# Stores of a decayed cumulative matmul: two queues for four lumps near the end, and half-size stores for the last chunk's lower lump

## The chip, the cores and the metric

The kernel runs on one core of a Trainium2 chip. The time is the device time of one execution in microseconds (us). Five engines work side by side, each in the order of its own instructions: TensorE (PE, with its weight loads as PEld), VectorE (DVE), ScalarE (ACT), GpSimd (POOL) and SyncE (SP). SP here only issues stores. DMAs issued by SP go through one queue (q1 in the profile), those issued by GpSimd through another (q0). SP's issues are not counted as busy time of an engine; GpSimd's are.

## What is computed

```
xw = x @ w                       # x: 16 x 2048 x 1024, w: 1024 x 1024, float32
out[:, 0, :] = xw[:, 0, :]
for t in range(1, S):            # S = 2048
    out[:, t, :] = decay * out[:, t - 1, :] + xw[:, t, :]
```

So each row of x is multiplied by w, and along the 2048 steps of a sequence each of the 1024 columns keeps a running sum that decays by its own factor.

## The kernel before

The 16 sequences are cut into 64 chunks of 512 steps. Two chunks make a group, except that the last two chunks (62 and 63) stand alone. For each group the 1024 output columns are cut into 8 tiles of 128, so there are 31 x 8 slots of 1024 steps and then 2 x 8 of 512 steps: 264 slots in all. The text counts the last ones from the end: slots -24 to -17 are the last group of two chunks, -16 to -9 are chunk 62, and -8 to -1 are chunk 63.

What one slot does, with the letters of the written order:

- TensorE computes the tile's matmuls into PSUM (`ps` or `spare`, L131), columns on the partitions and steps along the row. Eight matmuls of 512 steps take 1.73 us.
- A **paired** tile is scanned at half length. ScalarE copies PSUM to `xs` (p, L183) and scales its even steps (g, L169). GpSimd adds these to the odd steps: the **join** (j, L196). VectorE scans the odd steps with the squared decay (S, L201) into `so`. ScalarE scales the result (h, L169), and GpSimd adds it to the even steps: the **fill** (c, L246). A small write sets the element ahead of the first step, the **zero** (z): a memset on GpSimd at a sequence's start (L190), a copy on ScalarE otherwise (L192).
- A tile that isn't paired is scanned by VectorE straight from PSUM (S, L221). A list `flips` says for which slots the usual choice is turned round; of the last eight, -8, -6, -3, -2 and -1 aren't paired.
- The last column of `so` is kept for the next chunk (k, L250).
- VectorE transposes the tile into the output buffer `ot` in blocks of 32 x 32 (B for back, L258).

Four tiles share one `ot` buffer, and there are four such buffers in a ring. A buffer with its four tiles is a **lump** here: half of the columns, for one group or chunk. When the last of the four transposes has been put in the program, `Outlet.store` issues the lump's stores (L279), one for each quadrant of 32 partitions, in the order 0, 2, 1, 3. A store of a two-chunk lump is 512 KB, one of a single chunk 256 KB. Each moves pieces of 512 bytes, 1024 or 512 of them.

The last four tiles (-4 to -1) have no such buffer. Their end is the deed `V`: TensorE transposes them in blocks of 128 steps (L383), ScalarE and VectorE copy two blocks each out of PSUM (L387), and SP stores each block, 128 rows of 2 KB (L389).

The order of the instructions is the order in which the program is written; `pin` keeps it. For the first 34 slots and the last 20 it is written out by hand in `agenda`, one string of deeds for a slot, where `S-13` is the scan of slot -13; the slots between follow a rule (`usual`, `rest`). A deed that touches several engines puts one instruction in each one's order. A `B` that completes a lump also puts the lump's stores there, and each waits for the lump's last transpose on VectorE.

Loads of x are issued by GpSimd (L105), 256 KB each and 128 KB for the first two chunks, and are cast to bf16 on the way. The last one is issued at 824.5 us.

Of the kernel before, what the change touches and what calls it, by code (L numbers as in the profile page):

```python
# [14 lines left out]
def _ap(ap_obj: bass.AP, new_ap, extra_offset=0):  # L15
    return dataclasses.replace(
        ap_obj,
        ap=[list(p) for p in new_ap],
        offset=ap_obj.offset + extra_offset,
    )  # L20
# [5 lines left out]
def kernel(  # L26
# [26 lines left out]
    nc = tc.nc  # L53
    pin = tc.keep_in_program_order
    B, S, D = x.shape
# [3 lines left out]
    P = 32  # L59
# [6 lines left out]
    R = K // 2  # L66
    CH = D // 2
    CR = CH // NQ
# [7 lines left out]
    def ring(pool, name, count, shape, dtype=FP32):  # L76
        i = turns[name] = turns.get(name, -1) + 1
        return pool.tile(shape, dtype, name=f"{name}{i % count}")

    def quad(q):  # L80
        return slice(q * P, (q + 1) * P)
# [12 lines left out]
    def ot_tile(nj):  # L94
        return ring(sb, "ot", 4, [128, nj, CR])
# [29 lines left out]
    def matmul(ps, n, k, xt, t0=0, t1=TL, start=0, pairs=None):  # L125
        if pairs is None:
            rhs = xt[:, k // 2, k % 2, t0:t1]
        else:
            rhs = pairs[:, k // 2, t0 // P:t1 // P, :, k % 2].rearrange("p j i -> p (j i)")
        lhs = wsb[:, k, n].rearrange("p q i -> p (q i)")  # L130
        pin(nc.tensor.matmul(  # L131
            out=ps[:, t0:t1] if ps.shape[1] >= t1 else ps,
            lhsT=lhs,
            rhs=rhs,
            start=(k == 0 and t0 == start),
            stop=(k == K - 1),
        ))
# [3 lines left out]
    class Tile:  # L141
# [3 lines left out]
        def __init__(self, g, n, ps, outlets):  # L145
            self.b, self.t0 = chunks[g[0]]
            self.T = TL * len(g)
            self.n, self.ps, self.outlets = n, ps, outlets
            self.paired = n % R != R - 1
            if len(tiles) in flips or len(tiles) - len(slots) in flips:  # L150
                self.paired = not self.paired
            self.turn = len(tiles)
            self.lot = sum(t.paired for t in tiles)
            self.prev = None if self.t0 == 0 else last[n]
            if self.t0 + self.T < S:
                last[n] = const.tile([128, 1], FP32, name=f"keep{n}", bufs=2)
                self.keep = last[n]
            else:
                self.keep = None
# [106 lines left out]
    class Outlet:  # L266


        def __init__(self, ns, nj, half=0, queues=(nc.sync,)):
            self.ns, self.missing, self.half = ns, set(ns), half  # L270
            self.nj, self.t0, self.queues = nj, half * nj * P, queues
            self.ot = ot_tile(nj)

        def store(self, b, t0):
            n0 = self.ns[0]
            c0 = n0 % R * P
            size = len(self.ns) * P
            for i, q in enumerate((0, 2, 1, 3)):
                pin(self.queues[i % len(self.queues)].dma_start(  # L279
                    out=_ap(out, [[D, P], [P * D, self.nj], [1, size]],  # L280
                            (b * S + t0 + self.t0) * D + n0 // R * CH + q * CR + c0),
                    in_=self.ot[quad(q), :, c0:c0 + size]))

# [1 line left out]
    size = M * CH  # L287
# [37 lines left out]
    for q in range(NQ):  # L325
        pin(nc.sync.dma_start(
            out=rows[q * P:q * P + R],
            in_=_ap(decay, [[P, R], [CH, 2], [1, P]], q * CR)))
# [75 lines left out]
    def turn_and_load(c):  # L404
# [77 lines left out]
        -17: "h-20 k-20 c-20 S-18 k-18",  # L482
        -16: "I S-17 B-20 p-16 g-16 j-16",
        -15: "z-15 k-17 B-18 z-16",
        -14: "p-15 g-15 B-17 z-14 j-15",
        -13: "p-14 S-16 g-14 j-14 S-15 h-16 k-16 c-16",
        -12: "S-13 h-15 k-15 c-15 S-14 k-13",
        -11: "p-12 B-13 h-14 B-15 g-12 c-14 k-14 B-16",
# [1 line left out]
        -9: "p-10 k-12 g-10 h-12 B-11 j-10 k-11",  # L490
        -8: "S-9 c-12 S-10 k-9",
        -7: "z-7 B-12 h-10 k-10 B-9 c-10 S-8",
        -6: "p-7 g-7 B-10 j-7 B-8",
        -5: "S-7 S-6 h-7 c-7",
        -4: "z-4 S-5 B-7",
        -3: "p-4 B-6 g-4 B-5 j-4",
# [13 lines left out]
    def usual(s):  # L510
        paired = [t.paired for t in tiles]
        do = [f"P{s}"] if paired[s] else []
        if paired[s - 1]:
            do.append(f"S{s - 1}")
        if not paired[s]:
            do.append(f"S{s}")
        do.append(f"C{s - 1}")
        if paired[s - 2]:
            do.append(f"B{s - 2}")
        if not paired[s - 1]:  # L520
            do.append(f"B{s - 1}")
        return do + later.get(s, []) + ["L"] * (2 if len(loads) > NQ else 1)

    def rest(s):
        do = [f"S{s - 1}"] if tiles[s - 1].paired else []
        do.append(f"C{s - 1}")
        if tiles[s - 2].paired:
            do.append(f"B{s - 2}")
        return do + [f"B{s - 1}"] + later.get(s, []) + ["L"] * len(loads)

    def perform(do):
        for deed in do:
            deeds[deed[0]](int(deed[1:] or 0))
# [3 lines left out]
    for step, (g, n) in enumerate(slots):  # L537
        T = TL * len(g)
        left = step - len(slots)
        if n % R == 0:  # L540
            ns, nj = range(n, n + R), T // P
            outlets = [Outlet(ns, nj)]
        if left == -R:
            outlets = []
        if step == 0:
            heads = [ring(psp, "ps", 3, [128, T]) for _ in range(3)]
            firsts = [ps[:, 0:TL] for ps in heads] + [spares[0]]
            seconds = [ps[:, TL:T] for ps in heads] + [spares[1]]
            for j0, j1 in halves:
                for k in range(0, K, 2):  # L550
                    for i in range(R):
                        matmul(firsts[i], i, k, xt_of[0], j0 * P, j1 * P, pairs=xw_of[0])
            for k in range(1, K, 2):
                for i in range(R):
                    matmul(firsts[i], i, k, xt_of[0])
            for k0 in range(0, K, 2):
                for i in range(R):
                    for k in (k0, k0 + 1):
                        matmul(seconds[i], i, k, xt_of[1], 0, H * P,
                               pairs=xw_of[1] if k0 < 4 else None)  # L560
            for i in range(R):
                for k in range(K):
                    matmul(seconds[i], i, k, xt_of[1], H * P, TL, H * P,
                           pairs=xw_of[1] if i < 2 else None)
        if step < R:
            ps = heads[n] if n < 3 else tuple(spares)
        else:
            if step == K + 1:
                ps = nexts
            elif len(g) == 2 or n % R < 3:  # L570
                ps = ring(psp, "ps", 3, [128, T])
            else:
                ps = ring(psp, "spare", 1, [128, TL])
            todo = [(k, l) for k in range(K) for l in range(len(g))]
            if step < K:
                todo.sort(key=lambda kl: kl[0] % 2)
            elif step == K:
                todo = []
                nexts = ring(psp, "ps", 3, [128, T])
                for l in range(len(g)):  # L580
                    for i, both in enumerate((ps, nexts)):
                        for k in range(K):
                            matmul(both[:, l * TL:(l + 1) * TL], n + i, k, xt_of.get(g[l]),
                                   pairs=xw_of[g[l]] if g[l] in (3,) else None)
            elif step == K + 1:
                todo = []
            if left == -1:
                ps = tuple(both[:, t:t + TL // 2] for t, both in zip(
                    (0, TL // 2), (ps, ring(psp, "ps", 3, [128, TL]))))
                for t, half in zip((0, TL // 2), ps):  # L590
                    for k in range(K):
                        matmul(half, n, k, xt_of[g[0]], t, t + TL // 2, t)
                todo = []
            for k, l in todo:
                matmul(ps[:, l * TL:(l + 1) * TL], n, k, xt_of[g[l]])
        tiles.append(Tile(g, n, ps, outlets))
        do = agenda.get(step, agenda.get(left) if left >= -20 else None)
        if do is None:
            do = usual(step)
        else:  # L600
            do = do.split()
            if left == -20:
                do = rest(step) + do
        perform(do)
# [29 lines left out]
```

## Time and profile before

| what | value |
|---|---|
| time, median of 3 runs | 905.78 us (905.29 to 906.42) |
| profiled execution, first to last instruction (its span) | 903.1 us |
| median of the runs less that span | 2.7 us |
| TensorE busy, granted clock | 99% of the span, 0.999 |
| VectorE, ScalarE, GpSimd busy | 91%, 76%, 73% |
| moved by DMA | 204.77 MB, mean 227 GB/s |
| SP's stores of 512 KB, issue to landing | 248, median 10.9 us |
| SP's stores of 256 KB, issue to landing | 12, median 4.3 us |
| GpSimd's loads of 256 KB, issue to landing | 248, median 7.8 us |

The profiled execution's own total time isn't listed apart from its span; what lies around the span is taken from the median of the runs. Times in the views are microseconds from the span's start. A row of a timeline has the start, the length, the engine, the line with what it writes and reads, and in brackets the idle time before it with what ended that. Rows that follow each other closely are merged, with their number after an x.

### The profile page before, as it was taken

The page shows a single profiled execution, that of the slowest core. Times are in us where ns is not written, and L with a number is a line of the kernel's source. Part 1 is how long each engine was busy: PE and PEld are TensorE (multiplying, and loading weights), DVE is VectorE, ACT ScalarE, POOL GpSimd, SP SyncE. Part 2 cuts the span into 40 slices and gives each one's busy share as a digit, 9 for nine tenths or more (in the row PEclk, how much of TensorE's full clock was granted, in tenths as well). Part 3 has the DMA queues.
Part 4 walks back from the last instruction along what each step waited for, and adds up shares of the span by engine and source line. Part 5 has one row for each costly group of instructions (what it writes and reads, how often), then busy time and mean ns, then how long its engine had stood idle before and what let it go on. Part 6 is the DMA issues. An engine that isn't in the chain of part 4 may idle for free.

```text
span 903.1 us, 11998 instructions
## 1 busy us (share of the span) xinstructions
PE 891.9 (99%) x4119; PEld 411.1 (46%) x4201; DVE 825.3 (91%) x628; ACT 686.0 (76%) x955; POOL 656.6 (73%) x755
## 2 busy tenths in 40 slices
PE   9999999999999999999999999999999999999997
PEld 5444444444444444444444444444444444444444
DVE  4999998999999999999998999999999999999997
ACT  4889867777877877877778778778777787787742
POOL 7888678777767768677677677787777776776632
PEclk9999999999999999999999999999999999999999
DMA  9999999999999999999999999999999999999868
GB/s 194 197 215 217 233 225 210 215 234 240 257 243 237 245 258 253 247 251 249 222 236 227 223 231 229 228 226 230 228 233 224 235 230 223 229 230 210 176 142 236
DMA packets 402543, 204.77 MB, mean 227 GB/s; under 512 B 8753, under 2 KB 401457, under 8 KB 402481
## 3 DMA queue, kind: packets, MB, share of 16 engines
q1 hardware_dynamic: 265168, 134.76, 61.3%
q0 software_dynamic: 137024, 68.70, 56.6%
q8 instruction: 33, 0.54, 0.2%
q10 hardware_dynamic: 288, 0.52, 0.2%
q14 instruction: 30, 0.24, 0.1%
HBM read 138.42 MB, written 134.22 MB: 302 GB/s over the span
## 4 chain that ended last, share of the span: by engine, by line
PE 94%; DMA 2%; POOL 1%; issue 1%; DVE 1%; ACT 0%; DVEq 0%; POOLq 0%
PE ps L131 94%; DMA xb<-in_x_dram 2%; POOL xb L105 1%; PE spare L131 1%; POOL ot L295 1%; DVE xw L115 0%; ACT xt L123 0%; DVE so L201 0%; DVE ot L258 0%; PE spare L383 0%; ACT xs L183 0%; PE ps L383 0%; DVE h L387 0%; ACT h L169 0%; DVEq L115 0%
## 5 line engine op out<-in xcount | busy, mean ns | idle before, releaser
L131 PE MATMUL ps<-xt,wsb 128*128 128x512 bf16 x3942 | 863.5, 378 | 4.7 <-DVE wsb L302 0.4
L131 PEld LDWEIGHTS <-wsb 128*128 128x128 bf16 x4152 | 405.9, 98 | 479.8 <-ACT wsb L302 0.8
L196 POOL TENSOR_TENSOR xs<-h,xs 128x512 f32<-128x512 f32 (+1 forms) x190 | 242.7, 1277 | 189.1 <-ACT h L169 85.0
L183 ACT COPY xs<-ps 128x1024 f32<-128x1024 f32 (+1 forms) x190 | 189.2, 996 | 155.4 <-PE ps L131 145.1
L258 DVE STREAM_TRANSPOSE ot<-so 128x1024 f32<-128x1024 f32 (+1 forms) x260 | 300.0, 1191 | 2.1 <-POOL so L190 1.1
L246 POOL TENSOR_TENSOR so<-h,xs 128x512 f32<-128x512 f32 (+1 forms) x190 | 241.2, 1271 | 43.5 <-ACT h L169 27.9
L123 ACT COPY xt<-xw 128x2048 bf16<-128x2048 bf16 (+1 forms) x136 | 242.1, 1789 | 7.7 <-DVE xw L115 7.7
L105 POOL DMA_DIRECT2D xb<-in_x_dram x264 | 174.0, 660 | 3.0 <-DMA ot<-in_w_dram 0.9
L169 ACT ACTIVATE h<-so,dec 128x512 f32<-128x512 f32 (+1 forms) x190 | 145.3, 765 | 27.9 <-DVE so L201 24.6
L115 DVE STREAM_TRANSPOSE xw<-xb 128x2048 f32<-128x2048 f32 (+1 forms) x78 | 147.3, 1901 | 6.9 <-DMA xb<-in_x_dram 6.9
L201 DVE TENSOR_TENSOR_SCAN so<-spare,keep,xs 128x512 f32<-128x512 f32 (+1 forms) x97 | 119.9, 1239 | 26.8 <-POOL xs L196 26.5
L201 DVE TENSOR_TENSOR_SCAN so<-spare,xs 128x512 f32<-128x512 f32 x93 | 113.2, 1219 | 27.4 <-POOL xs L196 24.5
L169 ACT ACTIVATE h<-ps,dec 128x512 f32<-128x512 f32 (+1 forms) x190 | 130.0, 684 | 0.0
L221 DVE TENSOR_TENSOR_SCAN so<-dec,ps 128x1024 f32<-128x1024 f32 x34 | 76.8, 2260 | 1.0 <-ACT h L169 1.0
L221 DVE TENSOR_TENSOR_SCAN so<-dec,keep,ps 128x1024 f32<-128x1024 f32 (+1 forms) x35 | 76.0, 2171 | 0.3 <-issue 0.2
L250 ACT COPY keep<-so 128x1 f32<-128x1 f32 x136 | 25.3, 188 | 9.5 <-DVE so L221 9.0
L192 ACT COPY so<-keep 128x1 f32<-128x1 f32 x97 | 18.4, 191 | 2.5 <-DVE ot L258 2.3
L131 PE MATMUL ps<-xw,wsb 128*128 128x256 bf16 (+1 forms) x68 | 11.2, 301 | 0.0
L190 POOL MEMSET so<- 128x1 f32 x93 | 10.6, 116 | 0.6 <-DVE ot L258 0.6
L131 PE MATMUL spare<-xt,wsb 128*128 128x512 bf16 (+1 forms) x48 | 10.0, 335 | 0.0
L295 POOL DMA_DIRECT2D ot<-in_w_dram x12 | 6.5, 544 | 3.0 <-DMA xb<-in_x_dram 2.0
L320 PE MATMUL spare<-idle 128*128 128x512 bf16 x22 | 6.5, 466 | 1.2 <-DVE idle L310 1.2
(37 smaller groups left out, 36.4 us busy)
## 6 DMA issues: line engine op xcount, KB each, us to landing
out_dram<-ot SPq DMA_DIRECT2D x248, 512.0 KB, 10.9
xb<-in_x_dram POOLq DMA_DIRECT2D x248, 256.0 KB, 7.8
out_dram<-ot SPq DMA_DIRECT2D x12, 256.0 KB, 4.3
xb<-in_x_dram POOLq DMA_DIRECT2D x16, 128.0 KB, 5.6
ot<-in_w_dram POOLq DMA_DIRECT2D x12, 128.0 KB, 5.1
out_dram<-xb SPq DMA_DIRECT2D x3, 256.0 KB
ot<-in_w_dram ACTq DMA_DIRECT2D x2, 256.0 KB, 4.7
ot<-in_w_dram SPq DMA_DIRECT2D x2, 256.0 KB, 4.4
```

The source lines that it names most:

```text
L105: pin(nc.gpsimd.dma_start(out=xb_of[c][quad(q), j0:j1], in_=_ap(x, [[D, P], [P * D, j1 - j0], [1, CQ]], (b * S + t0 + j0 * P) * D + q * CQ)))
L115: pin(nc.vector.transpose(out=dst.rearrange("p (m j i) -> p j m i", m=M, i=P)[:, j0:j1, m0:m1], in_=src.rearrange("p (j m c) -> p j m c", ...
L123: pin(copy(out=xt_of[c][:, m0:m1, :, j0 * P:j1 * P], in_=src))
L131: pin(nc.tensor.matmul(out=ps[:, t0:t1] if ps.shape[1] >= t1 else ps, lhsT=lhs, rhs=rhs, start=(k == 0 and t0 == start), stop=(k == K - 1),))
L169: pin(nc.scalar.activation(out=h, in_=src, func=mybir.ActivationFunctionType.Copy, scale=dec[:, self.n:self.n + 1]))
L183: pin(nc.scalar.copy(out=self.xs, in_=self.ps))
L196: pin(nc.gpsimd.tensor_tensor(out=odds, in0=self.g, in1=odds, op=ALU.add))
L201: pin(nc.vector.tensor_tensor_scan(out=so[:, 3:T + 2:2], data0=squares[-1][:, n:n + 1].to_broadcast([128, T // 2]), data1=self.xs[:, 1:T:2 ...
L221: pin(nc.vector.tensor_tensor_scan(out=so[:, t + 2:t + 2 + size], data0=dec[:, n:n + 1].to_broadcast([128, size]), data1=ps, initial=befor ...
L246: pin(nc.gpsimd.tensor_tensor(out=self.so[:, 2:T + 2:2], in0=self.h, in1=self.xs[:, 0:T:2], op=ALU.add))
L250: pin(nc.scalar.copy(out=self.keep, in_=self.so[:, self.T + 1:self.T + 2]))
L258: pin(nc.vector.transpose(out=outlet.ot[:, :, c0:c0 + P], in_=self.so[:, 2 + t0:2 + t0 + nj * P].rearrange("p (i t) -> p i t", t=P)))
```

## The change

The constructor of `Outlet` takes a number of pieces, and `store` issues that many stores for each quadrant, one after the other along the steps. The stores of the four lumps of slots -24 to -9 go to SP's and GpSimd's queues in turn: SP has quadrants 0 and 1, GpSimd 2 and 3. The lump of slots -8 to -5 stays with SP, in two pieces: eight stores of 128 KB instead of four of 256. In the written order of slot -14, `B-17` goes behind `z-14` and `j-15`, and in that of slot -6, `B-10` goes behind `j-7`.

```diff
-        def __init__(self, ns, nj, half=0, queues=(nc.sync,)):
+        def __init__(self, ns, nj, half=0, queues=(nc.sync,), pieces=1):
+            self.pieces = pieces
...
-            for i, q in enumerate((0, 2, 1, 3)):
-                pin(self.queues[i % len(self.queues)].dma_start(
-                    out=_ap(out, [[D, P], [P * D, self.nj], [1, size]],
-                            (b * S + t0 + self.t0) * D + n0 // R * CH + q * CR + c0),
-                    in_=self.ot[quad(q), :, c0:c0 + size]))
+            nj = self.nj // self.pieces
+            for j in range(0, self.nj, nj):
+                for i, q in enumerate((0, 2, 1, 3)):
+                    pin(self.queues[i % len(self.queues)].dma_start(
+                        out=_ap(out, [[D, P], [P * D, nj], [1, size]],
+                                (b * S + t0 + self.t0 + j * P) * D
+                                + n0 // R * CH + q * CR + c0),
+                        in_=self.ot[quad(q), j:j + nj, c0:c0 + size]))
...
-        -14: "p-15 g-15 B-17 z-14 j-15",
+        -14: "p-15 g-15 z-14 j-15 B-17",
...
-        -6: "p-7 g-7 B-10 j-7 B-8",
+        -6: "p-7 g-7 j-7 B-10 B-8",
...
-            outlets = [Outlet(ns, nj)]
+            both = -6 * R <= left < -2 * R
+            outlets = [Outlet(ns, nj, queues=(nc.sync, nc.gpsimd) if both else (nc.sync,),
+                              pieces=2 if left == -2 * R else 1)]
```

In GpSimd's order of instructions this puts two stores behind the fill of slot -22, ahead of the zero and the join of slot -20; two behind the join of slot -15, ahead of that of slot -14; two behind the join of slot -12, ahead of that of slot -10; and two behind the join of slot -7, ahead of its fill. The orders of TensorE, VectorE and ScalarE are the same as before.

## The prediction

> **What bounds the kernel now.** I read four views in this order: the chain of work that ended last, VectorE's timeline, GpSimd's timeline, and the windows by stage. The chain first, from its last stretch of matmuls:
>
> ```profile
> 889.95 4.48 PE ps L131 x20
> 894.43 0.87 PE spare L131 x8
> 895.30 0.87 PE ps L131 x8
> 896.17 0.73 PE spare L383 x4
> 896.91 0.76 PE ps L383 x7
> 897.67 0.33 PE spare L383 x3
> 898.00 0.11 PE ps L383
> 898.11 0.12 PE spare L383
> 898.23 0.02 issue
> 898.26 0.69 DVE h L387
> ```
>
> TensorE runs without a hole until 896.17 us. The last 6.9 us of the 903.1 us span are a tail: transposes, four copies, four stores. The change touches no matmul, so it can act only on this tail, or spoil the stretch ahead of it by stalling an engine. VectorE is the one to watch (start, length, what, idle before):
>
> ```profile
> 862.08 2.29 DVE L221 TENSOR_TENSOR_SCAN so<-dec,ps 128x1024 f32<-128x1024 f32 x1 [0.98 <-ACT h L169]
> 864.29 1.20 DVE L201 TENSOR_TENSOR_SCAN so<-spare,xs 128x512 f32<-128x512 f32 x1
> ...
> 876.72 0.73 DVE L201 TENSOR_TENSOR_SCAN so<-spare,keep,xs 128x256 f32<-128x256 f32 x1
> ...
> 890.75 1.87 DVE L258 STREAM_TRANSPOSE ot<-so 128x512 f32<-128x512 f32 x3
> 892.79 1.28 DVE L221 TENSOR_TENSOR_SCAN so<-dec,keep,ps 128x512 f32<-128x512 f32 x1 [0.17 <-issue]
> ```
>
> From 862.08 to 892.62 no idle time is listed, so each stall of VectorE there reaches the scan at 892.79, slot -3's. Its matmuls end two slots of 1.73 us before 896.17, at 892.7, so this scan follows TensorE, and the 0.17 us ahead of it are all the slack there is. From 892.79 on VectorE is again back to back up to the copies, so what is lost before shifts the tail. GpSimd's rows, in which the stores are put:
>
> ```profile
> 871.33 0.74 POOL L196 TENSOR_TENSOR xs<-h,xs 128x256 f32<-128x256 f32 x1 [3.17 <-ACT so L192]
> 873.32 0.73 POOL L196 TENSOR_TENSOR xs<-h,xs 128x256 f32<-128x256 f32 x1 [1.25 <-ACT h L169]
> 874.78 0.74 POOL L196 TENSOR_TENSOR xs<-h,xs 128x256 f32<-128x256 f32 x1 [0.73 <-ACT h L169]
> 875.69 1.43 POOL L246 TENSOR_TENSOR so<-h,xs 128x256 f32<-128x256 f32 x2 [0.17 <-ACT keep L250]
> ```
>
> The windows by stage show the stores (PE, PEld, DVE, ACT, POOL busy with counts, clock, DMA share, GB/s):
>
> ```profile
> 893.00:895.00 2.00, 2.00 (x14) 1.23 (x13) 2.00 (x3) 0.25 (x1) 0.00 (x0) 1.00 0.84 159
> 895.00:898.40 3.40, 3.22 (x27) 2.52 (x25) 3.11 (x5) 1.12 (x3) 0.73 (x1) 1.00 0.97 236
> 898.40:901.60 3.20, 0.00 (x0) 0.00 (x0) 0.55 (x1) 0.33 (x1) 0.00 (x0) 1.00 0.90 334
> ```
>
> The reader sees three different loads. To 893 the DMA engines work off one backlog. In 893 to 895 they run at 159 GB/s, with the backlog gone: slot -8's lump starts into nearly empty queues. Then come its rest at 236 GB/s and the last four stores at 334.
>
> **What the earlier lumps' split brings: 0.** In the trace, the lump of slots -12 to -9, issued from 887.29, lands by 893.7, one engine's share at 894.3; the next lump's first store is issued at 892.65 and its packets flow from about 893.4. An issue into empty queues (874.39) also shows its first packets 0.7 to 0.8 us later, so at most some 0.2 us of this start were queueing, and buffers (four of `ot`) hold nobody up: VectorE lists no wait for a store. Draining the earlier lumps faster is thus off the path. Whether two queues drain faster at all, the windows with loads and stores together bound: over 815 to 835 us both queues moved 208 GB/s, against 221 over 874.3 to 893 with SP's alone. I take no difference. Bounds: -0.2, the queueing; and +0.8 if GpSimd's stores land as late as its loads (7.8 us after issue, the median). The fourth pair, issued by 889.05, would land at 896.8; of its 0.5 MB some 0.2 would then run beside slot -8's lump, 0.8 us at 236 GB/s.
>
> [...]
>
> **What the split costs: VectorE's stalls.** GpSimd takes instructions in order, so each pair of stores waits for the lump's last transpose on VectorE and holds what is queued behind. The price of an issue is in the row of L105 (ns min/median/max):
>
> ```profile
> L105 POOL DMA_DIRECT2D xb<-in_x_dram x264: 575/665/780, 1.3 to 824.5; - x132
> ```
>
> The 128 KB loads (256 pieces of 512 B) take 575, the 256 KB loads (512 pieces) 665: 90 ns for 256 pieces more. A 512 KB store has 1024 pieces, by this line 665 + 180 = 845 ns. No such issue is in the trace; the low bound is 575, the high one is proportional to pieces, 1330. I take 845, since the two L105 sizes lie almost flat. A GpSimd add directly behind an issue began at least 0.27 us after its end.
>
> - Pair 1 (slots -24 to -21), ready at 861.12: two issues, 1.69, end at 862.81; the memset of 0.10 and the join of slot -20 (1.29; it began at 861.31 before) end at 864.20. Its reader on VectorE is the scan at 864.29. Stall 0; between 0 and 0.93 (2 x 1.33 + 1.39 + 0.05 from 861.12, less 864.29).
> - Pair 2 (slots -20 to -17), ready at 874.38 and put behind the join of slot -15 (873.32): ends 876.07, plus 0.27 and 0.74 for slot -14's join, which was done at 875.52: 877.08, with 0.1 to its reader 877.18, against the scan at 876.72. Stall 0.46; bounds 0 (575: 876.64) and 1.43. The two adds of 875.69 go with it and are wanted no earlier.
> - Pair 3 (-16 to -13), 256 KB each, ready at 879.83 plus the stall, 880.3: 2 x 0.665 end at 881.6; slot -10's join, next, waited to 881.83 anyway. 0.
> - Pair 4 (-12 to -9), ready at 887.7: with the reorder slot -7's join is ahead of it; ends 889.05; slot -7's fill began at 889.13. 0, at most 0.1.
>
> Together 0.46, less the 0.17 idle: **+0.3 us**, bounds 0 (an added issue can't free a join earlier) and 2.2 (0.93 + 1.43 - 0.17). SP's halved issues save nothing on the path: the most is 0.45, the lump of slot -16, ready at 879.83 and issued at 880.28 behind the one before, and it drains with the backlog. Moving two deeds in the written order costs nothing: slot -14's zero is ScalarE's (0.19), and its join and slot -7's only move ahead of VectorE's transposes in program order, not past other GpSimd work.
>
> [...]
>
> **What the pieces bring: -0.4 us.** Slot -8's lump: SP issues four stores at 892.65, 893.01, 893.57 and 894.70 (0.3 to 1.2 us each); landings complete at 895.75, 896.76, 897.89 and 899.22. The first store's 512 packets go at 159 GB/s, each 46 ns; from the second on 27 ns. If that slow phase is due to one quadrant's store alone in the queues, halves shorten it from 1.6 to 0.8 us, and the lump ends 0.8 us sooner, most of it behind cover: the last four stores are issued at 897.56, 898.32, 898.78 and 899.27 because of the copies, and their packets start at 898.41, within the usual 0.85. What remains is one late DMA engine, whose share of the lump landed at 899.22 and which then lands its part of the last stores at 902.22, 0.43 behind the other fifteen (901.79). With the lump done sooner it catches up: -0.4. Bounds: 0 (the slow phase is no matter of size) and -0.9: the last store, issued at 899.27, would with 0.85 to its first packet, 0.67 for 128 packets on 16 engines of 84 ns and 0.5 to land be in at 901.3 instead of 902.2. The four more issues at 315 ns (the shortest of a store here) are no load: SP waits 1.5 us for the copies anyway.
>
> **Sum.** +0.3 - 0.4 = -0.1 us on a profiled span of 903.1. The median of the runs shown is 905.78, 2.7 above the span; I leave these 2.7 as they are: **905.7 us**.
>
> **Rivals.**
> - Costly issue (slower): the price goes by pieces, 1.33 us a store. Then slot -20's scan waits 0.93 and slot -14's 1.43, in all 2.36 - 0.17 - 0.4 = +1.8: 907.6. It decides from 0.85 us an issue on: beyond, each 0.1 costs 0.4. For it: no SBUF-to-HBM store of GpSimd is in the trace. Against it: the flat L105 row.
> - Tail cut in full (faster): no stall, and the last stores meet empty queues: -0.9, 904.9. For it: the last store's 2.95 us to land against the first one's 2.41. Against it: the four stores themselves keep the engines 90% busy.
> - Nothing lands: two queues and halves move the same bytes at the same rate on the same engines, and the late engine stays late (an instruction fetch of 0.97 us in the DMA rows at 896.75 delays one): 0 - 0 + 0.3: 906.1. For it: the equal GB/s above.
>
> **How the numbers follow.** Forecast 0.45 (own range 905.1 to 906.2, which is the runs' own spread), nothing lands 0.22, costly issue 0.18, tail cut 0.13, anything else 0.02. What a measurement can tell from no change is about 0.2%, 1.8 us. Faster by that needs more than the 0.9 of the tail: 0.03. Slower needs the costly issue at or above its price and no gain: 0.11. Same: 0.86. The range runs from the tail cut less 0.3 of spread, 904.6, to the costly issue, 907.6.
>
> **What would show it.** Right: VectorE without listed idle from 862 to 892 but for about 0.5 us before slot -14's scan, released by GpSimd's L196; GpSimd's store issues at about 0.85 and 0.67; matmuls ending at the same time; the last landing about 0.4 sooner after the last issue. Wrong: store issues of 1.3 us or more, idle before slot -20's scan, a hole in TensorE's row, GpSimd's stores of the fourth lump still running beside slot -8's lump, or a tail under 6 us.

## The result, and the profile after

The changed kernel takes **908.67 us** (908.18 to 909.01, 6 runs), the kernel before, measured beside it, 905.46 (905.21 to 906.42, 6 runs): a ratio of 1.0032 [1.0021, 1.0042], 3.2 us slower. The profiled span went from 903.1 to 907.2 us. The forecast was 905.7 with a range up to 907.6, so even the range was too low.

First the parts that the prediction spoke of. The whole timeline of this profile lies 0.54 us later than the one shown before the change, from well ahead of the first split store (VectorE's scan at 862.08 is now at 862.62); times below are compared less this 0.54. VectorE's timeline and GpSimd's, at slots -14 and -3:

```profile
876.19 1.25 DVE L221 TENSOR_TENSOR_SCAN so<-dec,keep,spare 128x512 f32<-128x512 f32 x1
877.66 0.75 DVE L201 TENSOR_TENSOR_SCAN so<-spare,keep,xs 128x256 f32<-128x256 f32 x1 [0.22 <-POOL xs L196]
...
893.62 1.24 DVE L221 TENSOR_TENSOR_SCAN so<-dec,keep,ps 128x512 f32<-128x512 f32 x1
```

```profile
875.30 1.56 POOL L282 DMA_DIRECT2D out_dram<-ot  x2 [0.59 <-DVE ot L258]
876.87 0.75 POOL L196 TENSOR_TENSOR xs<-h,xs 128x256 f32<-128x256 f32 x1
```

Two issues of 512 KB take 1.56 us, and the join of slot -14 comes out behind them, at 877.62. Its scan waits 0.22 us for it. The scan that stood at 892.79, with 0.17 idle ahead of it, is at 893.62 with none: 0.29 later net of the offset. The last copy ends at 899.73 instead of 898.95, so all of VectorE's loss that reaches the tail is 0.24 us. (Slot -20's scan is 0.1 later too, and the transposes behind slot -14's scan another 0.12; the rest of this went into the slack ahead of slot -3's scan.) The chain of waits still ends with the same instruction:

```profile
899.04 0.69 DVE h L391
```

The other 3.0 us or so come behind the copies, in SP's queue. SP's timeline, after and then before (start, length, line, count):

```profile
893.73 6.97 SPq L282 DMA_DIRECT2D out_dram<-ot  x8
900.80 1.45 SPq L393 DMA_DIRECT2D out_dram<-xb  x3
902.66 0.33 SPq L393 DMA_DIRECT2D out_dram<-h  x1
```

```profile
892.65 3.30 SPq L279 DMA_DIRECT2D out_dram<-ot  x4
897.56 1.62 SPq L389 DMA_DIRECT2D out_dram<-xb  x3
899.27 0.39 SPq L389 DMA_DIRECT2D out_dram<-h  x1
```

Before, SP was through with slot -8's lump at 895.95 and then waited 1.6 us for the first copy. Now the eight issues last until 900.70, and the four last stores, whose copies are ready from about 898.3 on, wait for SP instead. The eight issues took 0.32, 1.78, 0.97, 1.73, 0.45, 0.47, 0.47 and 0.46 us one by one: the second and the fourth alone hold SP 3.5 us. The last landing, at 902.22 before, is at 906.01, 3.25 later net of the offset.

Why SP gets stuck shows in the windows of the three stretches ahead of it (PE, PEld, DVE, ACT, POOL busy with counts, clock, DMA share, GB/s), after and then before:

```profile
875.00:882.00 7.00, 6.95 (x33) 3.15 (x33) 6.76 (x10) 4.26 (x15) 5.90 (x9) 1.00 0.73 144
882.00:888.00 6.00, 6.00 (x30) 2.74 (x28) 5.96 (x8) 2.73 (x9) 3.28 (x5) 1.00 0.99 199
888.00:893.00 5.00, 4.95 (x24) 2.25 (x23) 5.00 (x7) 1.57 (x4) 2.55 (x5) 1.00 1.00 213
```

```profile
875.00:882.00 7.00, 6.95 (x34) 3.14 (x33) 6.97 (x10) 4.58 (x15) 3.55 (x6) 1.00 0.86 194
882.00:888.00 6.00, 6.00 (x29) 2.70 (x28) 6.00 (x9) 2.06 (x8) 2.74 (x4) 1.00 0.98 251
888.00:893.00 5.00, 4.95 (x24) 2.28 (x24) 4.83 (x7) 1.57 (x4) 1.48 (x2) 1.00 1.01 253
```

The last two numbers carry it. The DMA engines are as busy as before (0.99 and 1.00 in the second and third window) but move a fifth and a sixth less. By 893 the changed kernel has moved 7 x 50 + 6 x 52 + 5 x 40 KB/us = 0.86 MB less, of which the offset explains some 0.14 (0.54 us at 253 GB/s). This backlog, bytes that had moved by then before and still have to move here, is 3.4 us of work at 253 GB/s, or 2.9 without the offset, and it now stands ahead of slot -8's lump. The prediction had counted on the earlier lumps' stores being gone by then.

### The profile page after: what moved, and what is told of

Read it like the earlier page. It is cut to its first block, busy times and chain, and to the rows that moved or that the text cites. A ratio compares the mean times of both kernels' runs of the same rounds, so it can differ in the third digit from the quotient of the medians.

```text
span 907.2 us, 12004 instructions
## 1 busy us (share of the span) xinstructions
PE 892.8 (98%) x4119; PEld 411.4 (45%) x4201; DVE 826.3 (91%) x628; ACT 686.2 (76%) x955; POOL 663.0 (73%) x763
## 4 chain that ended last, share of the span: by engine, by line
PE 93%; DMA 2%; POOL 1%; issue 1%; DVE 1%; ACT 0%; POOLq 0%; DVEq 0%
PE ps L131 93%; DMA xb<-in_x_dram 2%; POOL ot L299 1%; POOL xb L105 1%; PE spare L131 1%; DVE xw L115 0%; ACT xt L123 0%; ACT xs L183 0%; DVE so L201 0%; PE spare L387 0%; DVE ot L258 0%; ACT h L169 0%; PE ps L387 0%; POOLq L635 0%; POOL xs L196 0%
## 5 line engine op out<-in xcount | busy, mean ns | idle before, releaser
L105 POOL DMA_DIRECT2D xb<-in_x_dram x264 | 174.3, 661 | 3.3 <-DMA ot<-in_w_dram 1.1
L282 POOL DMA_DIRECT2D out_dram<-ot x8 | 5.7, 722 | 5.5 <-DVE ot L258 5.1
```

The source lines that it names most:

```text
L105: pin(nc.gpsimd.dma_start(out=xb_of[c][quad(q), j0:j1], in_=_ap(x, [[D, P], [P * D, j1 - j0], [1, CQ]], (b * S + t0 + j0 * P) * D + q * CQ)))
```

## The experiments

Each edit is told against the changed kernel. The ratios are against the kernel before, measured beside it (905.22 to 905.29 us).

| kernel | time, us | ratio [95%] | against before |
|---|---|---|---|
| e1_pieces_only | 905.57 | 1.0003 [0.9994, 1.0012] | +0.3 |
| e2_split_only | 907.61 | 1.0025 [1.0015, 1.0035] | +2.35 |
| e3_split_first_three | 907.42 | 1.0024 [1.0014, 1.0034] | +2.2 |
| e4_split_fourth_only | 905.70 | 1.0004 [0.9995, 1.0013] | +0.4 |
| e5_mixed_halves | 905.86 | 1.0005 [0.9996, 1.0013] | +0.6 |
| e6_sp_quadrants_in_order | 908.95 | 1.0039 [1.0027, 1.0052] | +3.7 |
| e7_gpsimd_alone | 907.58 | one run | +2.3 |
| e8_stall_alone | 906.11 | 1.0008 [0.9999, 1.0017] | +0.85 |
| e9_change_mixed_halves | 906.67 | 1.0015 [1.0007, 1.0024] | +1.4 |
| e10_second_lump_only | 906.24 | 1.0011 [1.0002, 1.0020] | +0.95 |
| e11_act_queue_at_end | 915.43 | 1.0113 [1.0097, 1.0128] | +10.1 |
| e12_one_store_ahead | 906.34 | one run | +1.1 |

**e1_pieces_only** and **e2_split_only** take the change apart.

```diff
-            both = -6 * R <= left < -2 * R
+            both = False                              # e1
...
-                              pieces=2 if left == -2 * R else 1)]
+                              pieces=1)]                # e2
```

> The changed kernel with all stores on SP again, so only the halved stores of slot -8's lump (and the two moved deeds, which are idle without the split) remain. Theory (GpSimd's half of the fourth lump starts some 4 us after its issue and takes the DMA engines from slot -8's lump, so SP can't issue the rest in time): 905.2 to 905.8, as before or up to 0.4 faster. Rival 'eight issues' (SP's eight stores, not the split, delay the last four): 907.5 to 908.7, SP's last four stores issued from about 900.

> The changed kernel with slot -8's lump in four stores of 256 KB again; the split of four lumps stays. Theory: 907.8 to 908.8, about as slow as the changed kernel, SP's issues for slot -8's lump again 1 to 2 us each. Rival 'eight issues': 905.7 to 906.2 (VectorE's 0.3 alone).

The pieces alone do nothing that can be measured; the split alone makes up 2.35 of the 3.2 us. Four issues instead of eight also get stuck in e2:

```profile
893.46 4.94 SPq L282 DMA_DIRECT2D out_dram<-ot  x4
```

They took 0.32, 1.70, 1.54 and 1.25 us, and the last four stores started at 898.50 instead of 897.56. The windows of e2 read 151, 210 and 211 GB/s, those of e1 185, 251 and 255. So the slower drain belongs to the split.

**e3_split_first_three** and **e4_split_fourth_only** (both with `pieces=1`) tested my first theory: that GpSimd's half of the fourth lump (slots -12 to -9) lands late and runs beside slot -8's lump.

```diff
+            both = -6 * R <= left < -3 * R            # e3
...
+            both = left == -3 * R                     # e4
```

> Lumps of slots -24, -20 and -16 split over the two queues, that of slot -12 on SP alone, slot -8's lump in four stores. GpSimd's stores have landed before slot -8's lump is issued. Theory: 905.7 to 906.2, since only VectorE's stall of about 0.5 less its 0.2 of slack is left. Rival 'stalls' (GpSimd's issues delay joins and through VectorE the end): 907.5 to 908.7, as all the stalls are in the first two pairs.

> Only the lump of slots -12 to -9 split, slot -8's lump in four stores. Theory: 907.5 to 908.7; GpSimd's packets of 4096 bytes run from about 892.5 to 897 beside slot -8's stores. Rival 'stalls': 905.3 to 905.8, no join waits behind this pair. Rival 'eight issues': the same.

The theory fell, and clearly: without the fourth lump's split all but 0.2 us of the loss is there (windows 142, 196, 224 GB/s), and with it alone only 0.4. The loss is made in the first three lumps, ahead of the tail, and carried as backlog. Of these the lump of slots -24 to -21 hands nothing on: split, it lands by 875.69, and the next lump's first packets flow at 875.88.

**e5_mixed_halves** and **e6_sp_quadrants_in_order** (both with `pieces=1`) tested the second theory. Taken in turn, the order 0, 2, 1, 3 gives SP quadrants 0 and 1, which are partitions 0 to 63, and GpSimd 2 and 3, partitions 64 to 127. The guess was that stores of one half of the partitions, one after the other, move slower than stores that change half: SP alone, going 0, 2, 1, 3, changes half at each store (251 GB/s over 882 to 888 in the kernel before), while in the changed kernel each queue keeps to one half (199). e5 gives each queue one quadrant of each half; e6 has no store on GpSimd at all and only sorts SP's quadrants, from slot -28's lump on.

```diff
-                for i, q in enumerate((0, 2, 1, 3)):
+                for i, q in enumerate((0, 2, 1, 3) if len(self.queues) == 1 else (0, 1, 2, 3)):                    # e5
+                for i, q in enumerate((0, 1, 2, 3) if len(tiles) > len(slots) - 6 * R else (0, 2, 1, 3)):          # e6
...
+            both = False                              # e6
```

> The split of four lumps as in the changed kernel, but SP has quadrants 0 and 2 and GpSimd 1 and 3, so each queue has stores from both halves of the partitions; slot -8's lump in four stores. Its twin is the run with the split alone (907.61). Theory 'halves' (a queue whose stores all read partitions 0 to 63, or all 64 to 127, moves at 175 to 180 GB/s; two halves together reach 250, and the changed kernel gave each queue one half, one after the other): SP's stores of slot -20's lump at over 200 GB/s, the backlog gone again by 894, 905.7 to 906.6. Rival 'GpSimd's late start' (its stores start only 4 to 7 us after their issue, whatever they read): GB/s from 875 to 882 below 165 as in the twin, 907.2 to 908.

> All stores on SP, slot -8's lump in four stores, but from slot -28's lump on in the order of quadrants 0, 1, 2, 3 instead of 0, 2, 1, 3: neighbours in the queue read the same half of the partitions. No GpSimd store, no stall. Theory 'halves': 150 to 190 GB/s from 875 to 882 against 194, under 235 from 882 to 888 against 251, a backlog ahead of slot -8's lump, 905.8 to 907.3. Rival 'GpSimd's late start': 905.0 to 905.6, no change.

Both times came out for the halves, e6 beyond what I had expected. Its windows, and then those of e5:

```profile
875.00:882.00 7.00, 6.95 (x33) 3.23 (x33) 7.00 (x10) 4.28 (x15) 3.62 (x5) 1.00 0.75 154
882.00:888.00 6.00, 6.00 (x30) 2.70 (x29) 5.97 (x9) 2.65 (x9) 2.70 (x4) 1.00 0.88 196
888.00:893.00 5.00, 4.95 (x24) 2.29 (x24) 5.00 (x7) 1.58 (x4) 1.23 (x3) 1.00 0.96 231
```

```profile
875.00:882.00 7.00, 6.95 (x33) 3.19 (x33) 6.76 (x11) 4.26 (x15) 5.81 (x9) 1.00 0.76 166
882.00:888.00 6.00, 6.00 (x30) 2.70 (x29) 5.96 (x8) 2.79 (x9) 3.28 (x5) 1.00 1.01 262
888.00:893.00 5.00, 4.95 (x24) 2.29 (x24) 5.00 (x7) 1.57 (x4) 2.53 (x5) 1.00 0.91 223
```

One queue, the same bytes, the same number of stores: sorting the quadrants takes the middle window from 251 to 196 GB/s, nearly the changed kernel's 199, with no GpSimd store and no stall. And mixing the halves in the two queues brings it back to 262. Between e2 and e5, which differ in nothing but which quadrants a queue has, lie 1.75 of the 2.35 us.

One part of e5's expectation failed: SP's two stores of slot -20's lump, quadrants 0 and 2, were to run at over 200 GB/s, and ran at 177 (876 to 878) and 166 (878 to 880). The rate in slices of 0.15 us, 876 to 882, shows why, in the kernel before, in e6 and in e5:

```profile
GB/s 177 177 177 174 177 188 164 174 177 184 174 171 157 143 130 239 300 259 259 239 215 208 195 174 171 171 174 164 160 167 198 229 259 273 273 273 270 259 253 242
```

```profile
GB/s 188 174 171 177 177 177 171 171 191 174 164 184 188 171 171 177 177 178 171 171 174 188 174 171 164 177 184 181 181 177 174 174 171 177 181 174 140 130 147 253
```

```profile
GB/s 181 174 167 184 174 177 171 177 181 177 174 174 188 174 164 143 116 102 106 119 82 116 167 256 266 270 266 249 232 222 201 174 181 164 188 201 273 277 300 386
```

Every first store, alone in the queue, runs at some 175. In the kernel before and in e5 the rate goes up to 260 to 300 about where the second store, of the other half, takes over, and comes down again; in e6, where the second store is of the same half, it stays at 175. So the gain seems to lie in the handovers from one half to the other, of which a pair has one, and a full queue many.

And a quadrant decides two things at once: which partitions a store reads, and which 512 bytes of each output row it writes. No run separates the two. That the order of the quadrants sets the rate is shown; that it does so by the halves of the partitions is argued, and so it is meant wherever the text speaks of halves.

The stretches with one half alone moved 170 to 180 GB/s here (178 over 864 to 868 in e6, with the DMA engines 99% busy). e5's pair gains little over that: above 200 GB/s for about 1.2 us. With more stores in SP's queue the gain is larger: 251 GB/s over 882 to 888 in the kernel before, where they alternate, against 196 in e6, where two of one half follow each other.

**e7_gpsimd_alone** and **e12_one_store_ahead** ask about the other thing that the DMA rows of the changed kernel show: GpSimd's stores mostly run not beside SP's but behind them. In e7 all four stores of the lump of slots -24 to -21 are GpSimd's; in e12 the first is SP's and the other three GpSimd's. Both have `pieces=1` and all other stores on SP.

```diff
+                              queues=(nc.gpsimd,) if left == -6 * R else (nc.sync,)                         # e7
...
+                              queues=(nc.sync,) + (nc.gpsimd,) * 3 if left == -6 * R else (nc.sync,)        # e12
```

> Slot -24's lump with all four stores on GpSimd, everything else on SP. One look at when GpSimd's packets start with SP's queue empty. Theory 'own latency': first packets some 7 us after the first issue, as in the changed kernel (861.93 to 868.9). Rival 'behind SP' (GpSimd's packets wait until SP's are through): about 2 us. In the time: four issues ahead of slot -20's join, VectorE 2 us late, 906.5 to 908 either way.

> Slot -24's lump with its first store (quadrant 0) on SP and the other three on GpSimd; everything else on SP. One look at when GpSimd's packets start with one store of SP's ahead instead of two (7.0 us after the issue in the changed kernel) or none (1.4 us). If GpSimd's stores wait for what SP has in its queue: 3 to 4 us after the issue, when SP's 512 KB are through at 175 GB/s. If it is a matter of chance or of the engine's own work: 1.4 or 7 us again. The time, with three issues ahead of slot -20's join: 906 to 907.5.

The DMA view by queue (packets, MB, share of the 16 engines), the changed kernel in 862 to 868 us and then in 869 to 874:

```profile
q1 hardware_dynamic: 1767, 0.90, 88.6%
```

```profile
q0 software_dynamic: 245, 0.94, 99.2%
q1 hardware_dynamic: 13, 0.00, 0.4%
```

GpSimd's first store was issued at 861.93, yet to 868 only SP's queue, q1, moves anything; GpSimd's first packet flows at 868.89, 6.96 us after the issue, when SP's two stores are through. At slot -17 it is 6.87 us (875.30 to 882.17). Then the same view of e7 and of e12, both 862 to 868:

```profile
q0 software_dynamic: 235, 0.90, 82.6%
```

```profile
q1 hardware_dynamic: 1040, 0.52, 54.2%
q0 software_dynamic: 122, 0.49, 38.1%
```

With no store of SP ahead, GpSimd's first packet came 1.38 us after its issue (e7), with one 3.80 us (e12), with two 6.9 us (the changed kernel). e4 shows that it is no rule that SP must be through: there GpSimd's pair was issued at 887.95 with some 0.68 MB of SP's stores ahead, its first packet came 1.93 us later, when 0.48 MB of that had moved, and both queues moved from then on (e4, 889.9 to 893):

```profile
q0 software_dynamic: 140, 0.49, 64.2%
q1 hardware_dynamic: 484, 0.24, 33.4%
```

So in these stretches the two queues largely take turns rather than add up (in the changed kernel q1 has 88.6% and q0 nothing over 862 to 868, 0.4% and 99.2% over 869 to 874), and in the changed kernel each has its half of the partitions for itself. The late start alone isn't the cause: e5 has it too (first packet at 867.98, 5.95 us after the issue) and loses 0.6 us in all. That the split is slow by the two together is argued. What makes GpSimd's stores wait is not settled by these runs.

**e8_stall_alone** puts VectorE's stall in without the stores: SP has all stores (one piece), and GpSimd makes three copies into a tile that nothing reads (extra work) where the changed kernel issues its first two pairs.

```diff
+            if len(slots) - 5 * R - 1 < len(tiles) < len(slots) - 3 * R and self.nj == 2 * NJ:
+                for j in (0, 4, 8):
+                    pin(nc.gpsimd.tensor_copy(
+                        out=idle.rearrange("p (j c) -> p j c", c=CR),
+                        in_=self.ot[:, j:j + 4, :]))
...
+            both = False
```

> All stores on SP in four pieces, but where the changed kernel's GpSimd issues the stores of slots -24's and -20's lumps it copies parts of the finished lump into an unused tile three times, 1.6 to 2.4 us, and so holds the joins behind it as long or longer. Theory (stalls are a small part): 905.5 to 906.1, VectorE's scan at slot -14 waits 0.2 to 1 us for GpSimd. Rival 'stalls': 907 to 908.5.

The copies take 1.97 us against 1.59 for a pair of issues; VectorE waits 0.17 us at slot -20 and 0.32 at slot -14, and the time rises by 0.85 us, with an interval of -0.1 to +1.5. Its last copy ends some 0.5 us later net of its offset, that of the changed kernel 0.24. So stalls of the changed kernel's size are worth less than 0.85 and can't be the cause of 3.2.

**e9_change_mixed_halves** is the whole change with e5's order: it asks whether the pieces cost something by themselves.

> The whole change, with the eight small stores, but SP has quadrants 0 and 2 and GpSimd 1 and 3. Theory 'halves': as the run with the mixed halves and four stores, 905.5 to 906.4; the small stores cost only where a backlog meets them. Rival 'pieces cost by themselves': 906.6 to 907.2, the 0.9 to 1.1 that lay between the change and its split alone.

906.67 is the rival's figure. The pieces, worth +0.3 (within its interval of zero) in e1, cost 0.8 us here against e5, and 0.9 in the changed kernel against e2. As far as these runs go, they cost only where a backlog stands ahead of them. SP's eight issues in e9 took 0.32, 1.02, 0.45, 0.47, 0.47, 0.47, 1.47 and 0.45 us, and behind the seventh, held from 896.98 to 898.45, the DMA engines went down to 116 GB/s (898 to 899). In the changed kernel the same happens at the end of the fourth issue (896.93 to 898.66) and behind it; the window there:

```profile
898.30:899.30 1.00, 0.71 (x7) 0.47 (x5) 0.82 (x2) 0.39 (x2) 0.00 (x0) 1.00 0.26 60
```

The engines stand three quarters idle at 60 GB/s, although SP has four stores of the lump left. An instruction fetch of 16 KB took 1.26 us here, from 897.04 on, and one took 1.30 in e9. In e1 the like fetch came at 897.33, after the last of the eight issues (896.53), and none was held. That the fetch is what holds SP is a guess: no run varied it. Nor is it shown how many stores SP can have outstanding: in e1 the fifth was issued at 894.85, ahead of the first landing at 895.16, in 0.47 us.

**e10_second_lump_only** splits only the lump of slots -20 to -17, with the halves as in the change and one piece.

```diff
+            both = left == -5 * R
```

> Only the lump of slots -20 to -17 split, quadrants as in the changed kernel, slot -8's lump in four stores. If this lump's 2 MB, moved one half after the other, make the backlog: GB/s from 875 to 882 near 150, 906.3 to 907.6. If the lumps behind it (1 MB each) are what matters: 905.5 to 906.0, VectorE's stall alone.

It fell between the two expectations. The backlog is made (146 and 203 GB/s in the first two windows) and then partly worked off (292 in the third). So this loss, made far ahead of the tail, costs about what is left of it at 893 (1.2 us less the offset, for a cost of 0.95).

**e11_act_queue_at_end** was meant to beat both kernels: no stores on GpSimd, quadrants 2 and 3 of slot -8's lump and the third of the last four stores issued by ScalarE.

```diff
+            both = left == -2 * R
+            outlets = [Outlet(ns, nj, queues=(nc.sync, nc.scalar) if both else (nc.sync,), pieces=1)]
...
-            pin(nc.sync.dma_start(
+            pin((nc.scalar if i == 2 else nc.sync).dma_start(
```

> A version meant to beat both: no GpSimd stores; slot -8's lump in four stores of which SP issues quadrants 0 and 1 and ScalarE 2 and 3, so the two halves move side by side from the start, and the third of the last four stores is issued by ScalarE right behind its own copy. Theory: the slow first store (159 GB/s for 1.6 us) goes, the last store is issued 0.3 sooner: 904.5 to 905.2 against 905.3. Rival: ScalarE's issues hold its scaling for slot -4 back: 905.5 to 906.5.

It is 10 us slower, and its SP has waits that the question was not about (in all, times, longest):

```profile
SPq L282 <- DMA out_dram<-ot: 11.4, 2, 10.8
SPq L282 <- DMA out_dram<-xb: 4.2, 1, 4.2
```

SP held the third store of slot -16's lump until 895.73, for the landing of other stores, and over 888 to 893 the DMA engines moved 1 GB/s. In the kernel before, no store of this lump or of those behind it waits for a landing; why some do here is not shown. Whether ScalarE's queue would shorten the tail stays open. No version tried beat the kernel before.

The windows give one number for each kernel, the bytes that are missing at 893 against the kernel before, worked out as above and turned into time at 253 GB/s. Each profile's timeline lies somewhat later than that of the kernel before, by 0.3 to 0.6 us (VectorE's scan at 862.08 there); the next column takes this off.

| kernel | GB/s in the three windows | missing at 893 | as time | less the offset | cost |
|---|---|---|---|---|---|
| before | 194, 251, 253 | | | | |
| e1 (pieces) | 185, 251, 255 | 0.05 MB | 0.2 us | -0.1 us | +0.3 us |
| e4 | 180, 248, 241 | 0.18 MB | 0.7 us | 0.3 us | +0.4 us |
| e5 | 166, 262, 223 | 0.28 MB | 1.1 us | 0.5 us | +0.6 us |
| e9 (pieces) | 177, 256, 221 | 0.25 MB | 1.0 us | 0.6 us | +1.4 us |
| e8 (stall, no split) | 174, 242, 244 | 0.24 MB | 0.9 us | 0.6 us | +0.85 us |
| e10 | 146, 203, 292 | 0.43 MB | 1.7 us | 1.2 us | +0.95 us |
| e6 | 154, 196, 231 | 0.72 MB | 2.8 us | 2.2 us | +3.7 us |
| e2 | 151, 210, 211 | 0.76 MB | 3.0 us | 2.7 us | +2.35 us |
| e3 | 142, 196, 224 | 0.84 MB | 3.3 us | 2.7 us | +2.2 us |
| after (pieces) | 144, 199, 213 | 0.86 MB | 3.4 us | 2.9 us | +3.2 us |

Where slot -8's lump is stored in one piece and in the usual order, the cost lies within 0.6 us of the backlog less the offset, and below it where that is large: before, SP had 1.6 us to spare ahead of the last four stores, and 893 to 898 ran at only 213 GB/s, so part is caught up. e6 lies above this because its slow order goes on in slot -8's lump (205 GB/s in 893 to 898, where e2 and e3 moved 263 and 257). e8 has no split: what is missing there comes of its late VectorE.

## Why the prediction was wrong, point by point

- **The bound and the tail: right.** TensorE has no hole, the tail sets the end, and VectorE's loss shifts it.
- **VectorE's stalls, +0.3: right in sum, in part by luck.** 0.24 us came through to the copies. On the way VectorE lost 0.10 at slot -20, put at 0, some 0.32 at slot -14, put at 0.46, and 0.12 in the transposes behind, not foreseen. The 0.27 us put between an issue and the add behind it isn't there: the trace before has such adds 0.01 us behind an issue of L105, and here slot -14's join starts at 876.87, as the pair ends. What made up for it is that GpSimd's first issue began 0.28 us behind SP's (875.30 against 875.02). Issues took 0.79 to 0.80 us for 512 KB and 0.65 for 256 KB, against 0.845 and 0.665 estimated from L105. The rival of the costly issue did not occur, though the time lies near its 907.6: a right number would have had a wrong cause.
- **"What the earlier lumps' split brings: 0": this step failed.** The sentence was "Draining the earlier lumps faster is thus off the path". It holds only in that direction. I asked whether two queues drain faster, never whether they could drain slower by enough to come onto the path, and of the split I weighed only the number of queues. What else it changes, which quadrants lie next to each other in a queue, I had listed and not priced. The bound of +0.8, from GpSimd's late landings, was made for the fourth lump alone; the runs show +2.35 for the whole split (e2), of which 1.75 go with the quadrants of each queue (e5) and at most a few tenths with the stall. The evidence that I took for "no difference", 208 against 221 GB/s, mixed GpSimd's loads with SP's alternating stores, and says nothing of two store queues with a half each.
- **"If that slow phase is due to one quadrant's store alone": the clue was there.** The 159 GB/s at 893 to 895 was read as a start-up phase that halves of a store would shorten. Slow phases of the same kind fill the changed kernel: 46 ns for a packet of 512 bytes in that row, 39 to 48 in the slow stretches of SP's queue, and 360 to 373 for GpSimd's 4096 bytes, which is 45 to 47 for each 512. Read as the rate of one half, the same row would have pointed to the loss: at 160 to 180 GB/s a lump of 2 MB takes 12 us instead of 8.
- **The pieces, -0.4: wrong.** The slow start did get faster in e1, 188 GB/s against 159 over its first 2 us, but the lump as a whole did not: 206 against 207 over 5.4 us (893.31 to 898.71 in e1, which takes in its offset, 893 to 898.4 before). So it didn't end sooner. Alone the pieces brought +0.3 with an interval that takes in zero (e1), and 0.8 to 0.9 of cost with the split (e9 against e5, the change against e2). "No load" for four more issues held as long as SP had 1.5 us to spare; with a backlog SP is the bound, its issues last to 900.70.
- **The base** was a little high as well: 905.78 was the median of 3 runs, 905.46 that of 6.
- **What would show it wrong** named GpSimd's fourth-lump stores running beside slot -8's lump. The sign appeared (GpSimd's packets flow until 897.2) but was not the cause: split alone (e4), that lump costs 0.4 us, and the loss was made in the lumps ahead of it.

## What to carry to other kernels

Before you split a run of stores over two queues, write down which partitions, and which parts of the output, each queue then moves one after the other: the order of the quadrants alone was worth 3.7 us here, more than everything that the split was supposed to touch. And "off the path" has two sides: ask by how much a drain that nobody waits for could become slower before somebody does, here about 1.6 us of SP's time. A small odd rate in a row of the profile (159 GB/s where 250 is usual) is worth a cause before it is worth a term of the sum.

## What the runs showed of the hardware that was not expected

- SP's 32-partition stores moved about 175 GB/s, 39 to 48 ns for a packet of 512 bytes, while a store was alone in the queue or next to one of the same half (e6, 864 to 868: 178), and about 250 GB/s, at a median of 27 ns a packet, with several stores queued that alternate (251 and 253 in the kernel before, 882 to 893). With few stores queued the rate rose, to 260 to 300, only around the change of half, and the first 6 us of a lump into an empty queue ran at 194 (before, 862 to 868).
- GpSimd's stores began 1.4 (e7), 3.8 (e12) and 6.9 us (the changed kernel) after their issue with none, one and two 512 KB stores of SP ahead of them, and 1.9 us after it in e4. Their packets have 4096 bytes and take 372 ns over 869 to 874 and 364 over 882.5 to 887 of the changed kernel (medians; about 200 in e5 from 868 to 874, where GpSimd's pair has a quadrant of each half), and while they ran in the changed kernel SP's queue got little: SP's two stores of 256 KB for slot -16's lump, 1024 packets in issues begun at 880.96 and 881.32, moved 20 packets in 882.5 to 887, where the kernel before moved 491 per us over 882 to 893.
- SP's first two issues of slot -8's lump took 0.32 and 0.51 us in the kernel before, the third and the fourth 1.09 and 1.24; behind the backlog of the changed kernel a store of 128 KB took up to 1.78 us to issue. In e1 eight stores of 128 KB with no backlog ahead went out in 0.32 to 0.48 us each.
